# Layer 2's recurrence: two pairs of heads in the same slot, three units apart, equal shapes side by side, 18 slots a period

## The chip, the cores and the metric

One core of a Trainium2 chip runs the whole kernel. The metric is the device time of one execution in microseconds (us). Lower is better.

## The reference

A four-layer recurrent decoder makes one inference step: 272 prompt rows (16 of them learned meta rows) and 8 sample sequences of 8 rows each, 336 rows of 1024 features. Layer 2, the one that is changed, is an RWKV-7 time mixer with 32 heads of 64 features. Cut to what matters:

```python
def rwkv_chunk(p, carry, xn, pos0):
    ...
    def step(s, inp):
        r_t, w_t, k_t, v_t, a_t, b_t = inp
        sa = jnp.einsum('bhvk,bhk->bhv', s, a_t)
        s = s * w_t[:, :, None, :] + sa[..., None] * b_t[:, :, None, :] + v_t[..., None] * k_t[:, :, None, :]
        return s, jnp.einsum('bhvk,bhk->bhv', s, r_t)

    s_new, y = lax.scan(step, s0.astype(F32), (tm(r), tm(decay), tm(k), tm(v), tm(-kk), tm(kk * a)))
    ...
    out = (yn + bonus).reshape(b, l, D_INNER).astype(xn.dtype) * g
    return (xn[:, -1].astype(x_prev.dtype), s_new.astype(s0.dtype)), out @ p['w_o']
```

All of it is float32. The state s of one head is 64 by 64.

## The kernel before

The 32 heads are 16 pairs; the two heads of a pair lie in the two halves of the 128 partitions. The 336 columns of a pair are cut into six units of 64 (the last one padded): unit 0 holds the 64 sample columns, units 1 to 5 the prompt. Inside a unit the time steps are solved in closed form by small matrix products that were made earlier; from unit to unit the state is carried on. This is `recur(p)`. For each unit u of a pair it does, in this order:

- pX: a matmul for each head (from the packed state and values `sv` and the stored products `G`) into one corner of the bank `pch`; ScalarE copies it out as `xs`. Units 2 to 5 contract over 128 partitions (the trace writes 128*64), units 0 and 1 over 64 (64*64). Unit 0 adds two more matmuls.
- pyR (units 2 to 5): a 64*64 matmul for each head, the state's part of the output, into `pY`; and `sd`, two activations of ScalarE that scale the old state.
- pA: a 64*64 matmul for each head from `xs` and `Z` into `pch`; ScalarE copies the two halves over the state in `sv`.
- pS (units 1 to 5): a 128*64 matmul for each head from the new `sv` into `pch`; VectorE adds `sd` with a decay and writes the state of the next unit (two operations). py: a 128*64 matmul for each head into `pY`. Unit 0 also has pyI, 64*64, the sample states' part of the output.

In the trace pX and pS both stand as `pch<-SV,Gr`, pA as `pch<-xs,Zr`, pyR as `pY<-Pr,SV`, py as `pY<-Gr,SV`. Every matmul of float32 has two passes, so two heads make four records ("x4"). Three groups of work go in between:

- `before(p)`, two pairs ahead: the projection `pvv` (24 matmuls of 128 by 128 weights on 336 columns, eight steps of three), two sets of twelve 32*32 matmuls (`pAZ`), the sample products pX0 in two halves of four 128*64 matmuls, ScalarE's copy of `pvv` to `s.v` (in the trace `VF<-pvv`), three transposes `pvt` of `s.v`, and copies.
- `sample(p)`: two products by GpSimd, two 128*64 matmuls `pD` on 512 columns, the sample states.
- `after(p)`: normalization and gate of the pair before: `pb`, `pm`, `pq` (128*128) and work on the other engines. `weights` splits the next projection's weight in two parts (`whi`, `wlo`), and in the first seven periods `lanes` runs an inversion on VectorE (`tmpi`, `LT`).

The order is written out by hand: `InOrder` keeps each engine's instructions in the order in which the program makes them. Time is cut into slots; `PLAN` says in which slot of a period each step of a helper is made. The recurrence of a pair runs over two periods. In each slot first the recurrence makes its step or steps, then the helpers make theirs:

```python
        for q in (p, p + 1):
            if 0 <= q < KE and t % 2 == q % 2:
                next(us[q])
        later(t)
```

So before, pair p (units 3 to 5) and pair p + 1 (units 0 to 2) take turns, the one in the even slots and the other in the odd ones, three steps a unit, 20 slots a period. There are 17 periods, numbered p = -1 to 15 here; p = -1 has one pair only, and in periods 14 and 15 the projection of layer 2's output stands where `before` stood.

Of the kernel before, what the change touches and what calls it, by code (L numbers as in the profile page):

```python
# [10 lines left out]
F32 = mybir.dt.float32  # L11
# [6 lines left out]
P = 128  # L18
# [3 lines left out]
KE = E // P  # L22
# [5 lines left out]
N = NSAM + NP  # L28
# [20 lines left out]
CH = 64  # L49
NU = 6  # L50
NB = 384
# [187 lines left out]
class K:  # L239
# [12 lines left out]
    "products": (9, 10, 11, 12, 13, 14, 15),  # L252
    "chain": (7, 8, 9, 11, 12, 13, 13, 17, 17, 18, 19, 21, 22, 23, 24),
    "mix": (9, 10, 11, 12, 12, 14, 16, 16),
    "slots": 20,
    "before": (0, 0, 0, 2, 3, 5, 6, 7, 8, 11, 11, 13, 14, 16, 18, 19),
    "weights": (6, 7, 8, 14),
    "after": (0, 3, 6, 9, 11, 16, 17, 19, 19, 21, 25),
    "lanes": (3, 5, 14, 16, 19),
    "pz": (0, 1, 2, 6, 8, 12, 12, 13),  # L260
    "begun": (14, 14, 15, 15, 16, 17, 18, 19),
    "last": (4, 5, 6, 7, 8, 9, 10, 11, 14, 15, 16, 17),
    "wlo": (0, 1, 0, 1, 0, 1, 0, 1, 0, 1),
    "fill": (2, 2, 2, 3, 2, 3, 3, 3, 3, 3, 3),
    "tail": (0, 0, 0, 1, 0, 1, 1, 1, 1, 1, 1),
    "sample": (6, 10, 18, 19, 19, 19),
}


# [159 lines left out]
def blocks(t):  # L429
    return [t[:, j] for j in range(t.shape[1])]  # L430
# [866 lines left out]
def layer2(k, O):  # L1297
    nc, tc, A = k.nc, k.tc, k.A
# [20 lines left out]
    ss = [slice(0, HD), slice(HD, P)]  # L1319
    vs = ss[::-1]  # L1320
# [274 lines left out]
    def plan(g, start, slots):  # L1595
        for t in slots:
            todo.setdefault(start + t, []).append(g)

    def later(t):
        for g in todo.pop(t, ()):  # L1600
            next(g, None)
# [4 lines left out]
    for n in range(2 * KE + 2):  # L1606
        p, t0 = n // 2, 8 * n
# [5 lines left out]
        if p == KE:  # L1613
            x = gh, gl
            pgs.append(out)
        else:
            x = xr if n % 2 else xk
# [44 lines left out]
    lanes = [invert(n) for n in range(1, 4 * KE * NU // P)]  # L1662
# [50 lines left out]
    def before(p, x=None):  # L1713

        s = st[p]
        if p:
            pvv = k.ps.tile([P, 512], F32, tag="mm", name="pvv")[:, :N]
            x = dense_steps(k, pvv, W[p], blocks(vh), blocks(vl))
        else:
            x = iter(())  # L1720
        ab = Ab[p % 2]
        for hp in range(2):
            nc.gpsimd.tensor_copy(ab[ss[hp], :, hp], s.A0[ss[hp]].rearrange("p w (b t) -> p b w t", t=TS))
        for _ in range(3):
            next(x, None)
            yield

        pAZ = k.ps.tile([P, 512], F32, tag="az", name="pAZ")
        n = NU * HB
        A_ = tw.tile([P, NU, HB], F32, tag="A_", name="A_", bufs=1)  # L1730
        for u in range(NU):
            for hp in range(2):
                nc.tensor.matmul(pAZ[low[hp], u * HB : (u + 1) * HB], s.L[top[hp], u], s.Z[top[hp], u, HB:], start=True, stop=True)
        yield
        for hp in range(2):
            nc.vector.tensor_copy(A_[low[hp]].rearrange("p u c -> p (u c)"), pAZ[low[hp], :n])
        yield
        next(x, None)
        yield
        for u in range(NU):  # L1740
            for hp in range(2):
                nc.tensor.matmul(pAZ[top[hp], n + u * HB : n + (u + 1) * HB], A_[low[hp], u], s.Z[low[hp], u, HB:], start=True, stop=True)
        yield
        next(x, None)
        for hp in range(2):
            nc.vector.tensor_copy(s.Z[top[hp], :, HB:], pAZ[top[hp], n : 2 * n].rearrange("p (u c) -> p u c", c=HB))
        yield
        for _ in range(3):
            next(x, None)
            yield  # L1750
        pX0 = k.ps.tile([P, 512], F32, tag="az", name="pX0")[:HD, : NS * 4 * TS]
        s.x0 = tw.tile([P, 2, NS, TS], F32, tag="x0", name="x0")
        for half in range(2):
            for b in range(half * NS // 2, (half + 1) * NS // 2):
                nc.tensor.matmul(pX0[:, b * 4 * TS : (b + 1) * 4 * TS], s.S0[:, b], ab[:, b].rearrange("p g w t -> p (g w t)"), start=True, stop=True)
            if half == 0:
                if p:
                    nc.scalar.copy(s.v[:, :N], pvv)
            yield
        pvt = k.ps.tile([P, 512], F32, tag="mm", name="pvt")[:, :NB]  # L1760
        for j in range(3):
            nc.tensor.transpose(pvt[:, j * P : (j + 1) * P], s.v[:, j * P : (j + 1) * P], k.ident)
        for hp in range(2):
            nc.scalar.copy(s.x0[vs[hp]].rearrange("p w b t -> p b w t"), pX0.rearrange("p (b g w t) -> p b g w t", g=2, w=2, t=TS)[:, :, hp])
        yield
        for j in range(2):
            for hp in range(2):
                nc.vector.tensor_copy(s.sv[vs[hp], j::2, hp], pvt[ss[j]].rearrange("p (u g c) -> p u g c", g=2, c=HD)[:, :, hp])
            yield

    NT = PLAN["slots"]

    def recur(p):

        s = st[p]
        sv, G = s.sv, s.G
        s.c = k.ps.tile([P, 512], F32, tag=f"c{p % 2}", name="pch")
        pX, pA, pS = (s.c[:, j * HD : (j + 1) * HD] for j in (0, 0, 1))
        for u in range(NU):
# [4 lines left out]
                    nc.tensor.matmul(pX[ss[hp]], s.x0[vs[hp], 1].rearrange("p b t -> p (b t)"), k.ident[vs[hp], vs[hp]], start=False, stop=True)  # L1784
            xs = tw.tile([P, HD], F32, tag="xs", name="xs", bufs=2)
            nc.scalar.copy(xs, pX)
            if u > 1:
                py = [s.Y[h, u * CH : (u + 1) * CH] for h in ss]
                sd = tw.tile([P, HD], F32, tag="sd", name="sd", bufs=2)
                for hp, h in enumerate(ss):  # L1790
                    nc.tensor.matmul(py[hp], sv[h, u, hp], s.R[h, u], start=True, stop=False)
                    nc.scalar.activation(sd[h], sv[h, u, hp], AF.Copy, scale=WC[h, p, NS + u - 1 : NS + u])
            yield
            for hp in range(2):
                nc.tensor.matmul(pA[ss[hp]], s.Z[ss[hp], u], xs[ss[hp]], start=True, stop=True)
            for hp, h in enumerate(ss):
                nc.scalar.copy(sv[h, u, hp], pA[h])
            yield
            if u > 0:
# [7 lines left out]
                for h, q in zip(ss, o):  # L1807
# [2 lines left out]
                        nc.vector.tensor_scalar(q, pS[h], d, None, op0=MUL)  # L1810
                    else:
                        nc.vector.scalar_tensor_tensor(q, pS[h], d, sd[h], op0=MUL, op1=ADD)
            if u == 0:
                s.Y = k.ps.tile([P, 512], F32, tag="Y", name="pY")[:, :NB]
            py = [s.Y[h, u * CH : (u + 1) * CH] for h in ss]
            if u == 0:
                for hp in range(2):
                    nc.tensor.matmul(py[hp], k.ident[vs[hp], vs[hp]], s.x0[vs[hp], 0].rearrange("p b t -> p (b t)"), start=True, stop=False)
            for hp in range(2):
                nc.tensor.matmul(py[hp], sv[:, u, hp], G[:, 1, hp, u], start=u == 1, stop=True)  # L1820
            if u == NU - 1:
                nc.sync.dma_start(O["wkv_p"][:, p], wo)
            yield
        for _ in range(NT - 3 * NU):
            yield

    def sample(p):
# [135 lines left out]
    todo, pz = {}, []  # L1963
# [9 lines left out]
    us, n_begun = {}, 0  # L1973
    for t in range((KE + 1) * NT):
        i, p = t % NT, t // NT - 1
        if i == 0:
# [20 lines left out]
                plan(sample(p + 1), t, PLAN["sample"])  # L1997
            if p < 6:
                plan(lanes[1], t, PLAN["lanes"])
        for q in (p, p + 1):  # L2000
            if 0 <= q < KE and t % 2 == q % 2:
                next(us[q])
        later(t)
        if p + 1 == KE:
            if i == PLAN["begun"][0]:
                begun = [dense_steps(k, pz[m], W[KE + j], yh, yl, k0) for j, m, k0 in ((3, 2, 0), (2, 0, 8))]
# [10 lines left out]
    lanes = [weights(KE + 6), weights(KE + 7)]  # L2017
# [319 lines left out]
```

## Time and profile before

| | |
|---|---|
| time, median of 3 runs | 1894.67 us (1892.24 to 1909.81) |
| the profiled execution: its own time, its span | 1909.75 us, 1908.0 us |
| mean granted TensorE clock, share of 2.4 GHz | 0.952 |
| busy share of the span: TensorE matmul, VectorE, ScalarE, GpSimd | 93%, 62%, 41%, 34% |
| the chain that ended last: TensorE, VectorE, ScalarE | 77%, 10%, 4% |

The engines run side by side, each through its own list. PE is TensorE's matmuls, PEld its weight loads, DVE VectorE, ACT ScalarE, POOL GpSimd. The chain that ended last is followed back from the last instruction, at each step to what released it.

### The profile page before, as it was taken

What the parts mean: (1) busy time and instruction counts of PE and PEld (TensorE: products, weight loads), DVE (VectorE), ACT (ScalarE), POOL (GpSimd) and SP (SyncE); (2) the same over time, 40 slices, a digit from 0 to 9 for tenths busy, and PEclk for the clock granted to TensorE, in tenths of its full rate; (3) what the DMA queues carried; (4) which work ended last, traced back from release to release, by engine and by line L of the source; (5) the groups of instructions that cost most, each with busy time, mean ns of one, the idle gap of its engine ahead of it and who ended that gap; (6) DMA issues with size and microseconds to landing.
All of it is one profiled execution on the core that took longest, in us unless ns stands there. A gap on an engine that the chain in (4) does not pass through costs nothing.

```text
span 1908.0 us, 31685 instructions
## 1 busy us (share of the span) xinstructions
PE 1775.5 (93%) x11822; PEld 1358.8 (71%) x11822; DVE 1191.0 (62%) x2234; ACT 780.7 (41%) x1789; POOL 647.9 (34%) x853
## 2 busy tenths in 40 slices
PE   5998897999789997999998999999998899999997
PEld 3665696766469996666666876677778667677777
DVE  8989546499945456556876847665545635355444
ACT  2553244321044343444345354576664324232332
POOL 5667335200000035343434333343446313132212
PEclk9999898999989998999997998899999899999999
DMA  5564544554554442356655855455524466566552
GB/s 191 139 176 129 126 145 151 174 173 137 147 135 159 141 147 77 112 188 196 188 184 167 243 174 160 141 171 179 160 90 150 135 205 206 190 196 223 173 177 73
DMA packets 198698, 306.63 MB, mean 161 GB/s; under 512 B 115504, under 2 KB 132656, under 8 KB 196048
## 3 DMA queue, kind: packets, MB, share of 16 engines
q1 hardware_dynamic: 177584, 265.86, 45.9%
q0 software_dynamic: 10400, 32.72, 5.3%
q10 hardware_dynamic: 10560, 6.03, 1.1%
q8 instruction: 93, 1.52, 0.3%
q14 instruction: 61, 0.50, 0.1%
HBM read 225.31 MB, written 79.24 MB: 160 GB/s over the span
## 4 chain that ended last, share of the span: by engine, by line
PE 77%; DVE 10%; ACT 4%; issue 3%; DMA 2%; POOL 2%; SPq 1%; ACTq 0%; POOLq 0%; DVEq 0%
PE pg L382 8%; PE pkr L382 8%; PE pu L382 6%; PE pz L448 4%; PE pz L449 4%; PE pz L450 4%; PE pgm L382 4%; PE pch L382 4%; PE pvv L382 4%; PE py L2234 3%; PE pz L382 2%; PE py L382 2%; PE pY L382 2%; PE pn L2246 1%; PE pg L448 1%
## 5 line engine op out<-in xcount | busy, mean ns | idle before, releaser
L411 DVE TENSOR_TENSOR wlo<-wst,whi 128x1024 fp32r<-128x1024 f32 x138 | 170.8, 1238 | 140.9 <-ACT whi L407 106.9
L407 ACT CAST whi<-wst 128x1024 fp32r<-128x1024 f32 (+1 forms) x125 | 129.3, 1035 | 104.8 <-PE pr L450 51.2
L382 PE MATMUL pg<-x_n,wst 128*128 128x336 f32 x512 | 163.5, 464 | 0.0
L382 POOL TENSOR_TENSOR wlo<-wst,whi 128x512 fp32r<-128x512 f32 (+1 forms) x57 | 76.2, 1338 | 159.3 <-ACT whi L382 156.2
L382 PEld LDWEIGHTS pg<-x_n,wst 128*128 128x128 f32 x512 | 94.5, 193 | 43.9 <-issue 2.5
L2247 DVE SCALAR_TENSOR_TENSOR s<-s,pn 128x512 f32<-128x512 f32 x64 | 44.0, 687 | 126.0 <-PE pn L2246 126.0
L382 PE MATMUL pu<-x_n,wst 128*128 128x336 f32 x352 | 115.0, 467 | 2.4 <-DVE x_n L491 1.8
L382 PE MATMUL pkr<-xr,wst 128*128 128x336 f32 x256 | 99.2, 484 | 0.0
L382 PEld LDWEIGHTS pu<-x_n,wst 128*128 128x128 f32 x352 | 67.6, 198 | 36.2 <-issue 3.2
L382 PEld LDWEIGHTS pgm<-AR,BK 64*128 64x128 f32 x384 | 59.6, 194 | 45.4 <-issue 25.3
L382 ACT CAST whi<-wst 128x256 fp32r<-128x256 f32 (+1 forms) x117 | 67.0, 586 | 51.0 <-issue 13.4
L382 DVE TENSOR_TENSOR G<-pgm,gmask 128x128 f32<-128x128 f32 x192 | 46.4, 284 | 63.2 <-PE pgm L382 63.0
L382 PE MATMUL pgm<-AR,BK 64*128 64x128 f32 x384 | 82.2, 321 | 1.3 <-ACT G L382 1.3
L569 POOL TENSOR_TENSOR sums<-sums 128x336 f32<-128x336 f32 x19 | 22.6, 1203 | 167.8 <-ACT sums L567 164.4
L382 PE MATMUL pkr<-xk,wst 128*128 128x336 f32 x256 | 75.9, 446 | 0.0
L2248 POOL DMA_DIRECT2D out_ret_s<-s x32 | 17.3, 540 | 165.2 <-DVE s L2247 157.8
L382 PEld LDWEIGHTS pch<-SV,Gr 128*64 128x64 f32 (+1 forms) x704 | 38.7, 141 | 43.3 <-DVE SV L382 13.4
L382 PE MATMUL pch<-SV,Gr 128*64 128x64 f32 (+1 forms) x704 | 63.1, 251 | 6.8 <-DVE SV L382 5.1
L450 PE MATMUL pz<-gh,whi 128*128 128x336 f32 x208 | 65.9, 317 | 0.0
L449 PE MATMUL pz<-gl,whi 128*128 128x336 f32 x208 | 65.8, 316 | 0.0
L448 PE MATMUL pz<-gh,wlo 128*128 128x336 f32 x208 | 65.8, 316 | 0.0
L382 PEld LDWEIGHTS pkr<-xk,wst 128*128 128x128 f32 x256 | 48.6, 190 | 23.7
(779 smaller groups left out, 5337.3 us busy)
## 6 DMA issues: line engine op xcount, KB each, us to landing
wst<-in_l_in SPq DMA_DIRECT2D x64, 512.0 KB, 3.9
dG<-G SPq DMA_DIRECT2D x16, 1152.0 KB, 5.2
s<-in_l_s SPq DMA_DIRECT2D x33, 512.0 KB, 3.6
wst<-in_l_out SPq DMA_DIRECT2D x32, 512.0 KB, 3.8
wst<-in_l_glu SPq DMA_DIRECT2D x32, 512.0 KB, 3.7
wst<-in_l_g SPq DMA_DIRECT2D x32, 512.0 KB, 4.3
wst<-in_l_v SPq DMA_DIRECT2D x32, 512.0 KB, 4.8
out_ret_s<-s POOLq DMA_DIRECT2D x32, 512.0 KB, 3.9
```

The lines of the kernel that those rows point to most:

```text
L382: return lambda *a, **kw: tc.keep_in_program_order(getattr(e, name)(*a, **kw))
L407: k.nc.scalar.copy(hf, st)
L411: e.tensor_tensor(lf[:, a:b], st[:, a:b], hf[:, a:b].bitcast(F32), op=ALU.subtract)
L448: k.nc.tensor.matmul(out, lo[:, j, :], xh[kk], start=first, stop=False)
L449: k.nc.tensor.matmul(out, hi[:, j, :], xl[kk], start=False, stop=False)
L450: k.nc.tensor.matmul(out, hi[:, j, :], xh[kk], start=False, stop=last)
L569: (nc.vector if m == KD - 1 and name != "xx" else nc.gpsimd).tensor_tensor(sums[name], sums[name], t, op=ADD)
L2234: nc.tensor.matmul(read.py0[32 * c : 32 * c + 32], qs[:, d, b], states[h * NS + b][:, d], start=d == 0, stop=d == 1)
L2246: nc.tensor.matmul(pn, KS[r, j, d * P : (d + 1) * P], VS[r, j], start=True, stop=True)
L2247: nc.vector.scalar_tensor_tensor(s[:, d], s[:, d], math.exp(TS * LOG_G[h]), pn, op0=MUL, op1=ADD)
L2248: nc.gpsimd.dma_start(O["ret_s"][h, b], s)
```

## The change

`recur` now has six steps a unit and not three. In each even slot both pairs make two steps in turn: p, p + 1, p, p + 1; in odd slots neither makes one. A unit still takes three even slots: first pX of both pairs, then `sd` of both; next pA of both, then pyR or pyI and the copies to `sv` of both; last pS and the state of both, then py of both. pyR stood next to pX and now stands behind pA. A period has 18 slots. `before` gets one more step: two projection steps are now made between the halves of pX0, and the copy of `pvv` to `s.v` is made behind the second half, not the first. The slots of all helpers are set anew.

```diff
--- before.py
+++ after.py
@@ -252,18 +252,18 @@
     "products": (9, 10, 11, 12, 13, 14, 15),
     "chain": (7, 8, 9, 11, 12, 13, 13, 17, 17, 18, 19, 21, 22, 23, 24),
     "mix": (9, 10, 11, 12, 12, 14, 16, 16),
-    "slots": 20,
-    "before": (0, 0, 0, 2, 3, 5, 6, 7, 8, 11, 11, 13, 14, 16, 18, 19),
-    "weights": (6, 7, 8, 14),
-    "after": (0, 3, 6, 9, 11, 16, 17, 19, 19, 21, 25),
-    "lanes": (3, 5, 14, 16, 19),
-    "pz": (0, 1, 2, 6, 8, 12, 12, 13),
-    "begun": (14, 14, 15, 15, 16, 17, 18, 19),
+    "slots": 18,
+    "before": (1, 1, 2, 3, 5, 5, 7, 8, 9, 9, 10, 11, 11, 12, 13, 14, 15),
+    "weights": (5, 7, 8, 13),
+    "after": (0, 3, 4, 9, 10, 15, 16, 17, 17, 19, 22),
+    "lanes": (3, 5, 9, 11, 17),
+    "pz": (1, 1, 5, 5, 7, 9, 11, 13),
+    "begun": (13, 13, 15, 15, 16, 16, 17, 17),
     "last": (4, 5, 6, 7, 8, 9, 10, 11, 14, 15, 16, 17),
     "wlo": (0, 1, 0, 1, 0, 1, 0, 1, 0, 1),
     "fill": (2, 2, 2, 3, 2, 3, 3, 3, 3, 3, 3),
     "tail": (0, 0, 0, 1, 0, 1, 1, 1, 1, 1, 1),
-    "sample": (6, 10, 18, 19, 19, 19),
+    "sample": (4, 7, 16, 16, 17, 17),
 }
 
 
@@ -1721,7 +1721,7 @@
         ab = Ab[p % 2]
         for hp in range(2):
             nc.gpsimd.tensor_copy(ab[ss[hp], :, hp], s.A0[ss[hp]].rearrange("p w (b t) -> p b w t", t=TS))
-        for _ in range(3):
+        for _ in range(2):
             next(x, None)
             yield
 
@@ -1735,27 +1735,29 @@
         for hp in range(2):
             nc.vector.tensor_copy(A_[low[hp]].rearrange("p u c -> p (u c)"), pAZ[low[hp], :n])
         yield
-        next(x, None)
-        yield
+        for _ in range(3):
+            next(x, None)
+            yield
         for u in range(NU):
             for hp in range(2):
                 nc.tensor.matmul(pAZ[top[hp], n + u * HB : n + (u + 1) * HB], A_[low[hp], u], s.Z[low[hp], u, HB:], start=True, stop=True)
         yield
-        next(x, None)
         for hp in range(2):
             nc.vector.tensor_copy(s.Z[top[hp], :, HB:], pAZ[top[hp], n : 2 * n].rearrange("p (u c) -> p u c", c=HB))
         yield
-        for _ in range(3):
-            next(x, None)
-            yield
+        next(x, None)
+        yield
         pX0 = k.ps.tile([P, 512], F32, tag="az", name="pX0")[:HD, : NS * 4 * TS]
         s.x0 = tw.tile([P, 2, NS, TS], F32, tag="x0", name="x0")
         for half in range(2):
             for b in range(half * NS // 2, (half + 1) * NS // 2):
                 nc.tensor.matmul(pX0[:, b * 4 * TS : (b + 1) * 4 * TS], s.S0[:, b], ab[:, b].rearrange("p g w t -> p (g w t)"), start=True, stop=True)
             if half == 0:
-                if p:
-                    nc.scalar.copy(s.v[:, :N], pvv)
+                for _ in range(2):
+                    yield
+                    next(x, None)
+            elif p:
+                nc.scalar.copy(s.v[:, :N], pvv)
             yield
         pvt = k.ps.tile([P, 512], F32, tag="mm", name="pvt")[:, :NB]
         for j in range(3):
@@ -1784,15 +1786,23 @@
                     nc.tensor.matmul(pX[ss[hp]], s.x0[vs[hp], 1].rearrange("p b t -> p (b t)"), k.ident[vs[hp], vs[hp]], start=False, stop=True)
             xs = tw.tile([P, HD], F32, tag="xs", name="xs", bufs=2)
             nc.scalar.copy(xs, pX)
+            yield
+            if u == 0:
+                s.Y = k.ps.tile([P, 512], F32, tag="Y", name="pY")[:, :NB]
+            py = [s.Y[h, u * CH : (u + 1) * CH] for h in ss]
             if u > 1:
-                py = [s.Y[h, u * CH : (u + 1) * CH] for h in ss]
                 sd = tw.tile([P, HD], F32, tag="sd", name="sd", bufs=2)
                 for hp, h in enumerate(ss):
-                    nc.tensor.matmul(py[hp], sv[h, u, hp], s.R[h, u], start=True, stop=False)
                     nc.scalar.activation(sd[h], sv[h, u, hp], AF.Copy, scale=WC[h, p, NS + u - 1 : NS + u])
             yield
             for hp in range(2):
                 nc.tensor.matmul(pA[ss[hp]], s.Z[ss[hp], u], xs[ss[hp]], start=True, stop=True)
+            yield
+            for hp, h in enumerate(ss):
+                if u > 1:
+                    nc.tensor.matmul(py[hp], sv[h, u, hp], s.R[h, u], start=True, stop=False)
+                if u == 0:
+                    nc.tensor.matmul(py[hp], k.ident[vs[hp], vs[hp]], s.x0[vs[hp], 0].rearrange("p b t -> p (b t)"), start=True, stop=False)
             for hp, h in enumerate(ss):
                 nc.scalar.copy(sv[h, u, hp], pA[h])
             yield
@@ -1810,18 +1820,11 @@
                         nc.vector.tensor_scalar(q, pS[h], d, None, op0=MUL)
                     else:
                         nc.vector.scalar_tensor_tensor(q, pS[h], d, sd[h], op0=MUL, op1=ADD)
-            if u == 0:
-                s.Y = k.ps.tile([P, 512], F32, tag="Y", name="pY")[:, :NB]
-            py = [s.Y[h, u * CH : (u + 1) * CH] for h in ss]
-            if u == 0:
-                for hp in range(2):
-                    nc.tensor.matmul(py[hp], k.ident[vs[hp], vs[hp]], s.x0[vs[hp], 0].rearrange("p b t -> p (b t)"), start=True, stop=False)
+            yield
             for hp in range(2):
                 nc.tensor.matmul(py[hp], sv[:, u, hp], G[:, 1, hp, u], start=u == 1, stop=True)
             if u == NU - 1:
                 nc.sync.dma_start(O["wkv_p"][:, p], wo)
-            yield
-        for _ in range(NT - 3 * NU):
             yield
 
     def sample(p):
@@ -1997,9 +2000,11 @@
                 plan(sample(p + 1), t, PLAN["sample"])
             if p < 6:
                 plan(lanes[1], t, PLAN["lanes"])
-        for q in (p, p + 1):
-            if 0 <= q < KE and t % 2 == q % 2:
-                next(us[q])
+
+        for _ in range(2 - 2 * (i % 2)):
+            for q in (p, p + 1):
+                if 0 <= q < KE:
+                    next(us[q])
         later(t)
         if p + 1 == KE:
             if i == PLAN["begun"][0]:
```

## Rows read from the trace of the kernel before

**Rows 1.** Busy time by engine: the recurrence, then two periods without `lanes`; PEclk, DMA share, GB/s last.
```profile
core 0: us, PE busy (x) PEld busy (x) DVE busy (x) ACT busy (x) POOL busy (x), PEclk, DMA share, GB/s
...
1118.00:1427.00 309.00, 298.64 (x3512) 218.75 (x3512) 183.17 (x458) 189.89 (x646) 120.55 (x130) 0.93 0.48 147
...
1316.55:1349.84 33.29, 33.12 (x437) 24.03 (x435) 19.44 (x51) 22.31 (x79) 14.05 (x16) 1.00 0.57 179
```

**Rows 2.** Timeline of PE in one period: start, length, instruction, count.
```profile
1309.59 0.29 PE L382 MATMUL pY<-Gr,SV 128*64 128x64 f32 x4
1309.71 0.29 PE L382 MATMUL pch<-SV,Gr 128*64 128x64 f32 x4
...
1310.19 0.42 PE L382 MATMUL pvv<-xvh,wlo 128*128 128x336 f32 x1
...
1311.31 0.34 PE L382 MATMUL pch<-SV,Gr 128*64 128x64 f32 x4
1311.57 0.33 PE L382 MATMUL pY<-Pr,SV 64*64 64x64 f32 x4
1311.73 0.28 PE L382 MATMUL pch<-xs,Zr 64*64 64x64 f32 x4
1311.95 0.65 PE L382 MATMUL pX<-Ab,S 128*64 128x32 f32 x8
1312.53 0.33 PE L382 MATMUL pch<-xs,Zr 64*64 64x64 f32 x4
...
1314.22 0.55 PE L382 MATMUL pvt<-ident,VF 128*128 128x128 f32 x3
```

**Rows 3.** Timeline of ACT in the same period.
```profile
1311.73 0.20 ACT L382 COPY xs<-pch 128x64 f32<-128x64 f32 x1
1311.83 0.71 ACT L382 ACTIVATE sd<-SV,WC 64x64 f32<-64x64 f32 x2
1312.57 0.42 ACT L382 COPY SV<-pch 64x64 f32<-64x64 f32 x2
1313.02 0.44 ACT L382 COPY VF<-pvv 128x336 f32<-128x336 f32 x1
...
1313.81 0.41 ACT L382 CAST whi<-wst 128x256 fp32r<-128x256 f32 x1
1314.24 0.53 ACT L382 COPY x<-pX 64x128 f32<-64x128 f32 x2
```

**Rows 4.** Timeline of DVE early in the recurrence.
```profile
1167.60 0.74 DVE L382 TENSOR_TENSOR tmpi<-LT 128x255 f32<-128x255 f32 x1
1168.38 1.15 DVE L382 TENSOR_TENSOR LT<-LT,tmpi 128x255 f32<-128x255 f32 x1
...
1169.87 0.57 DVE L382 SCALAR_TENSOR_TENSOR SV<-pch,WC,sd 64x64 f32<-64x64 f32 x2
```

**Rows 5.** Timeline of PEld, its longest waits in the recurrence; in brackets idle time and releaser.
```profile
1146.86 0.20 PEld L382 LDWEIGHTS pch<-SV,Gr 128*64 128x64 f32 x4 [1.61 <-DVE SV L382]
...
1170.49 0.20 PEld L382 LDWEIGHTS pch<-SV,Gr 128*64 128x64 f32 x4 [1.70 <-DVE SV L382]
...
1212.07 0.20 PEld L382 LDWEIGHTS pch<-SV,Gr 128*64 128x64 f32 x4 [1.53 <-DVE SV L382]
...
1240.67 0.19 PEld L382 LDWEIGHTS pch<-xs,Zr 64*64 64x64 f32 x4 [1.84 <-ACT xs L382]
...
1407.26 0.29 PEld L382 LDWEIGHTS pch<-SV,Gr 128*64 128x64 f32 x4 [2.15 <-DVE SV L382]
```

**Rows 6.** Busy time in stretches of one granted clock each.
```profile
1120.00:1171.60 51.60, 48.21 (x651) 34.72 (x650) 36.38 (x92) 27.89 (x103) 21.16 (x23) 1.00 0.48 142
1171.80:1188.70 16.90, 16.90 (x133) 12.32 (x132) 8.46 (x23) 7.78 (x26) 3.53 (x3) 0.50 0.30 76
...
1212.70:1229.60 16.90, 16.90 (x135) 12.99 (x136) 7.05 (x22) 8.11 (x28) 3.56 (x4) 0.50 0.37 103
1229.80:1407.10 177.30, 172.08 (x2166) 122.86 (x2164) 103.77 (x263) 120.88 (x413) 75.20 (x83) 1.00 0.50 159
1407.30:1413.90 6.60, 6.60 (x35) 5.42 (x35) 1.23 (x3) 4.17 (x13) 2.91 (x3) 0.50 0.53 165
```

## The prediction

> **What bounds the kernel now.** I read the stretch of the recurrence first, 309 us of the 1908.0 us span, for nothing else is touched. TensorE is busy in 298.64 of the 309.00 us, ScalarE in 189.89, VectorE in 183.17 [rows 1]. Two periods late in the stretch, without the inversion on VectorE, take 33.29 us, 16.64 a period, with TensorE busy in 33.12 [rows 1]: there TensorE's list sets the time and everything else hides beside it. So I read next how TensorE's list costs its time, in the order of its starts [rows 2]. What is to be seen is that the price of two small matmuls hangs on their neighbours. A group of four records between two others of another tile shape takes 0.26 us to the next start (1311.31 to 1311.57). The first of two groups of one shape takes 0.16 (1311.57 to 1311.73), the last 0.22 (1311.73 to 1311.95), one in the middle 0.12 (1309.59 to 1309.71). Two groups side by side thus take 0.38 and apart 0.52: each change of shape that goes saves 0.14 us. Last I read ScalarE's list in the same period [rows 3], because the change moves its instructions, and the longest waits of TensorE with the clock behind them [rows 5, 6].
>
> **What is removed: changes of shape.** I wrote TensorE's list of a period out from the slots, before and after, and counted the places where a matmul's tile shape differs from that of the one ahead. Before there are 32 and 30 in turn. After there are 20: pA of both pairs, pyR and pyI stand in one run, pS and py of both in another, the halves of pX0 and both pD stand beside 128*64 groups. Periods 0 to 13 lose 154 changes, the three at the ends 22, together 505 to 329. 172 of the 176 lie between small shapes; the visits to 128*128 stay eight a period. 176 x 0.14 = **24.6 us** if nothing else becomes late; in a period of the middle 11 x 0.14 = 1.54. At half clock a change costs more, so this errs low by little.
>
> **What is moved: ScalarE's order in slots 12 to 14.** Here I find the gain again as a wait. In slot 12 the recurrence makes pX of both pairs (units 5 and 2) and their two `xs`, then `sd` of both, which is four activations. Only behind them does `before` make the second half of pX0 and the copy of `pvv` to `s.v`. In slot 13 stands `pvt`, which reads `s.v`, and behind it on TensorE is everything of slots 14 to 16. Count from the start T of that pX. The first `xs` starts 0.42 later (1311.31 on TensorE to 1311.73 on ScalarE, [rows 2, 3]; ScalarE had work until then, so at most that). The second follows some 0.12 later, T + 0.54, as its group ends so much later. `sd` starts 0.10 behind an `xs` (1311.73 to 1311.83) and two take 0.72 with their gap: four are out at T + 0.64 + 1.44 = T + 2.08. The copy takes 0.44 [rows 3]: T + 2.52. A released matmul starts 0.05 later (two state updates end at 1169.87 + 0.57 = 1170.44, the matmul behind them starts at 1170.49, [rows 4, 5]): `pvt` at T + 2.57. TensorE gets there at T + 0.16 + 0.12 for the two pX and 0.58 for the half of pX0 (1311.95 to 1312.53, [rows 2]), T + 0.86. It waits **1.71 us**. Before, one pair's two `sd` stood ahead of the copy, and it ended at 1313.46, 0.76 ahead of `pvt` at 1314.22 [rows 2, 3]: a wait of that kind did not exist.
>
> Behind the wait come `pvt` (about 0.46, estimated from three matmuls and a change of shape), four 64*64 groups (0.16 + 0.12 + 0.12 + 0.22 = 0.62) and `pq` (about 0.5, from six matmuls of 336 columns in 1.12, 1310.19 to 1311.31), so pS of pair p could start at T + 4.15 and that of p + 1 0.16 later. ScalarE's `whi` (0.41) and `x` (0.53) are done by T + 3.5, but the four copies to `sv` cannot start before the third 64*64 group is done, now that pyR reads the old state just ahead of them: about T + 3.75, and two take 0.42. The second pair is released near T + 4.6, a wait of 0.3. Together **2.0 us a period**, in the 14 periods that have both pairs and a `pvt`: 28 us. Bounds: 1.2 (the two `xs` earlier, the second wait gone) to 2.2, so 17 to 31.
>
> **What is moved and hides.** In slots 0 and 6 only pair p has `sd`, and the same walk leaves pA 0.7 us to spare; VectorE's state update ends 0.5 us and more ahead of the next pX; pX behind the last pS is covered by py and both pD, about 1.5 us, to within 0.1. SyncE's loads stay at slot 0, and a period of about the same length brings none closer to its use; `wkv_p` goes out a step later, read by nobody: 0. GpSimd's list keeps its order but for `sample`, whose products are now ready well before `pD`: 0. If one of these covers failed, the price is one of 0.1 to 0.5 a period, 1 to 7 us. VectorE's inversion has its steps in other slots. One step takes up to 0.74 + 1.15 = 1.89 [rows 4] and delays a state update behind it, both before and after. I take 0, bounds -6 and +6: one such step less or more on the way in the three periods with the large ones.
>
> **The sum, and the clock.** Without the clock: -24.6 + 28 = +3.4. The profiled execution took 1909.75 us, 1908.0 of span and 1.75 around it, 15 over the median of 1894.67. Rows 6 show two stretches of the recurrence at a granted clock of 0.50 (1.2 GHz) of about 17 us each. There TensorE started 133 matmuls in 16.90 us, 7.9 per us, against 437 / 33.29 = 13.1 at 2.4 GHz [rows 1, 6]: 16.9 x (1 - 7.9 / 13.1) = 6.7 us lost in each, 13.4 in both, close to the 15. I therefore make the sum on 1909.75 - 13.4 = 1896.4, and take the median, 1894.7, as a run without them. What went ahead of them: five times in this stretch the weight load stood idle for over 1.5 us [rows 5]. Behind 1170.49, 1212.07 and 1407.26 the clock fell to 0.50 within a us or two, behind 1146.86 and 1240.67 it stayed at 1.00 [rows 5, 6]. The change puts 14 waits of that length in, one a period, with short matmuls around them, so falls are likelier than before. I take one more than in the median run: 1894.7 + 3.4 + 6.7 = 1904.8, **1905 us**.
>
> A rule of the Trainium skill speaks against the change here. The page "TensorE: Matmul & The Clock Gate", Part 3, "The mechanism", says that matmuls start and end strictly in program order, only weight loads being pulled ahead. By that rule nothing of slots 14 to 16 can fill the wait for `s.v`, which stays whole. The five waits agree: the weight load itself stood still up to 2.15 us.
>
> **The rivals.** (1) **The clock falls often, slower.** The mechanism is the wait for `s.v` once a period, and then 1.2 GHz for some 17 us, about one period. For: three of five such waits did it. Against: at half clock TensorE gets to `pvt` later and the wait shrinks, and some falls were short (6.6 us at 1407.3). Every second or third wait of the 14 makes five falls: 1894.7 + 3.4 + 5 x 6.7 = 1932. It decides from the third fall on (1918). (2) **The wait does not bind, faster.** If `s.v` is ready when TensorE comes to `pvt`, because ScalarE has run ahead or a later matmul goes first, the 24.6 stays: 1870; with 0.7 of the wait left, 1880. For: TensorE's busy share, and that ScalarE is busy only 22.31 of 33.29 us. Against: ScalarE's list is in program order [rows 3], and `xs` cannot be earlier than its pX, so there is nothing to run ahead with. (3) **The price of a change of shape is not saved**, because waits for data and the drain overlapped: then +28 without the gain, 1922, in the slower case.
>
> **How the numbers follow.** A measurement of this kernel can tell about 1% from no change, 19 us: 1876 to 1914. The main case, gain and wait about equal and at most two falls, spans 1885 to 1913 and has 0.42. The slower cases, 1914 to 1945, have 0.38; the faster, 1862 to 1876, have 0.20. Of these I leave out the ends: 1868 to 1938, which also takes in the bounds of the wait (17 to 31) and of the inversion (-6 to +6).
>
> **What would show it.** Right: TensorE's count of matmuls unchanged, groups at 0.12 in runs of four; `pvt` with an idle of 1.5 to 1.9 us ahead, released by ScalarE's `VF`; in a full-clock period 16.5 to 17.1 us. The clock's row tells the case. Wrong: `pvt` without a wait and a period near 15.1 us would mean that I put ScalarE's queue wrongly; a period over 18 us at full clock, another cover that failed, most likely VectorE's state update or the copies to `sv`.

## The result and the profile after

The changed kernel takes 1929.66 us (median of 4 runs, 1925.10 to 1931.09), the kernel before 1897.85 beside it: a ratio of 1.0128 on record, with a 95% interval of 1.0092 to 1.0164. (The eight times themselves give 1.0155 by their means and 1.0168 by their medians; the four of before are spread over 17.6 us.) Run again beside other runs of before, as `after_again` below, it stands at 1.0120 (1.0073 to 1.0167). It is slower by 1.2 to 1.7%, and inside the range that was given. The profiled execution took 1931.09 us, with a span of 1929.3 and a mean granted clock of 0.946. Its span is 21.3 us longer than that of before; from the first to the last matmul into `pch`, 22.7 us longer. So the recurrence is the place, as before. First its windows before and after, columns as in [rows 1]:

```profile
1118.50:1423.60 305.10, 294.74 (x3487) 215.03 (x3487) 181.43 (x455) 187.95 (x641) 119.52 (x129) 0.93 0.48 148
```

```profile
1115.80:1443.60 327.80, 277.50 (x3487) 206.62 (x3487) 181.04 (x455) 192.31 (x641) 120.91 (x129) 0.90 0.45 138
```

TensorE does the same 3487 matmuls in 17.2 us less busy time. But the time in which it stands idle goes from 305.10 - 294.74 = 10.4 to 50.3 us: 39.9 more. And the mean clock falls from 0.93 to 0.90. With two levels, 1.00 and 0.50, that is a share of 0.14 and then 0.20 of the stage at 1.2 GHz, 43 and 66 us. What TensorE waited for in the stage after (total in us, times, longest):

```profile
PE pvt L382 <- ACT VF L382: 25.5, 15, 2.2
PE pY L382 <- DVE cl L382: 9.2, 11, 2.3
PE pch L382 <- ACT SV L382: 9.1, 19, 1.2
PE pch L382 <- DVE SV L382: 2.8, 8, 0.6
PE pch L382 <- ACT xs L382: 1.7, 2, 1.2
```

In before the same view has 5.1 us for the state update, 1.6 for `xs`, 0.7 for the copies to `SV`, and neither of the first two rows. The first row is the predicted wait. The second was not predicted: pyI writes the bank `pY`, which is free only when VectorE's `cl` of the pair before has read it. One late period on TensorE (start, length, in brackets idle time and releaser), to be set beside [rows 2]:

```profile
1300.99 0.45 PE L382 MATMUL pch<-SV,Gr 128*64 128x64 f32 x8
1301.27 0.60 PE L382 MATMUL pX<-Ab,S 128*64 128x32 f32 x8
1303.59 0.55 PE L382 MATMUL pvt<-ident,VF 128*128 128x128 f32 x3 [1.72 <-ACT VF L382]
1304.07 0.61 PE L382 MATMUL pch<-xs,Zr 64*64 64x64 f32 x8
1304.46 0.65 PE L382 MATMUL pY<-Pr,SV 64*64 64x64 f32 x8
1305.46 0.65 PE L382 MATMUL pch<-cl,ob 128*128 128x336 f32 x1 [0.36 <-ACT SV L382]
```

and ScalarE in the same place, beside [rows 3]:

```profile
1301.37 0.35 ACT L382 COPY xs<-pch 128x64 f32<-128x64 f32 x2 [1.49 <-PE pch L382]
1301.62 1.46 ACT L382 ACTIVATE sd<-SV,WC 64x64 f32<-64x64 f32 x4
1303.10 0.44 ACT L382 COPY VF<-pvv 128x336 f32<-128x336 f32 x1
```

Both pX stand side by side now, as one group of 8 in 0.28 us (1300.99 to 1301.27), where before each of them stood alone at 0.26 or as a first at 0.16. But with T = 1300.99 the four `sd` end at T + 2.09 and the copy `VF` at T + 2.55, and `pvt` starts at T + 2.60. It could have started at T + 0.88.

The clock, in short stretches around this `pvt` and the next:

```profile
1303.80:1304.10 0.30, 0.30 (x5) 0.13 (x3) 0.00 (x0) 0.28 (x2) 0.06 (x1) 1.00 0.00 0
1304.30:1310.80 6.50, 6.14 (x53) 4.08 (x50) 4.16 (x11) 3.01 (x11) 1.89 (x3) 0.50 0.58 157
1311.20:1323.09 11.89, 10.17 (x161) 8.06 (x160) 5.14 (x14) 7.46 (x27) 4.46 (x6) 1.00 0.52 163
...
1324.80:1327.90 3.10, 3.10 (x22) 1.74 (x24) 1.47 (x5) 1.32 (x4) 0.01 (x1) 0.50 0.86 229
```

TensorE stands idle for 1.72 us, starts `pvt` at 2.4 GHz, and within 0.6 us of that start the clock is at 1.2 GHz for some 7 us. A period later the same, for some 3.4 us. In the whole stage there are 14 such falls, and 12 of them begin within 2.5 us of the start of one of the 16 `pvt`. The other two come with an idle of 2.33 us at pyI and one of 1.19 us at the last `pq`. None is as long as the stretches of 17 us of before [rows 6]. A late period takes 18.7 to 19.9 us, against 16.64 [rows 1].

### The profile page after: what moved, and what is told of

It is laid out like the page before. It is cut to its first block, busy times and chain, and to the rows that moved or that the text cites. A ratio compares the mean times of both kernels' runs of the same rounds, so it can differ in the third digit from the quotient of the medians.

```text
span 1929.3 us, 31775 instructions
## 1 busy us (share of the span) xinstructions
PE 1757.9 (91%) x11822; PEld 1350.1 (70%) x11822; DVE 1190.1 (62%) x2234; ACT 785.6 (41%) x1789; POOL 646.0 (33%) x853
## 3 DMA queue, kind: packets, MB, share of 16 engines
q8 instruction: 93, 1.52, 0.3%
## 4 chain that ended last, share of the span: by engine, by line
PE 73%; DVE 12%; ACT 6%; issue 4%; DMA 2%; POOL 2%; SPq 0%; ACTq 0%; DVEq 0%; POOLq 0%
PE pg L382 8%; PE pkr L382 8%; PE pu L382 6%; PE pz L448 4%; PE pz L449 4%; PE pz L450 4%; PE pgm L382 4%; PE pch L382 3%; PE py L2239 3%; PE pvv L382 2%; PE pz L382 2%; PE py L382 2%; PE pn L2251 1%; PE pg L448 1%; PE pv L382 1%
## 5 line engine op out<-in xcount | busy, mean ns | idle before, releaser
L382 PE MATMUL pch<-SV,Gr 128*64 128x64 f32 (+1 forms) x704 | 53.4, 260 | 4.9 <-DVE SV L382 2.8
```

Source lines behind the costliest of these rows:

```text
L382: return lambda *a, **kw: tc.keep_in_program_order(getattr(e, name)(*a, **kw))
```

## The experiments

Three questions were open. Is it the waits alone, or the falls of the clock as well, and does the one bring the other? What stands next when the wait for `s.v` is taken away? And is the gain from fewer changes of shape there at all? Each expectation says in its own words which theories it tells apart. Edits are against the changed kernel. What is called a late period here runs from one `pvt` to the next, behind the last step of `lanes`.

**after_again**: the changed kernel as it is, for the spread of its falls.

> The changed kernel as it is, on the chip of these runs, for comparison: 1.009 to 1.016 of the kernel before, a fall of the clock in nearly every period.

1928.82 us; the stage again 327.7 us, the mean clock in it again 0.90, with 12 falls. Two late periods in a row had no fall, with the same wait of 1.72 us at `pvt`:

```profile
1345.60:1363.30 17.70, 14.88 (x217) 11.17 (x218) 9.33 (x25) 11.31 (x40) 7.00 (x8) 1.00 0.61 169
1363.30:1381.00 17.70, 14.89 (x217) 11.18 (x217) 9.33 (x25) 11.29 (x40) 7.00 (x8) 1.00 0.51 164
```

This separates the terms within one execution. At 2.4 GHz TensorE is busy for 14.88 us where it was 33.12 / 2 = 16.56 [rows 1]: 1.68 us gained a period. It is idle for 2.82: 1.72 at `pvt`, 0.46 at `pq`, 0.51 at pyI by its rows, and some 0.15 at the next pX. Waits cost more than shapes give back, by 17.70 - 16.64 = 1.06 us. And a period with a fall takes 18.7 (a short one) to 19.9 (a long one), so the fall costs another 1.0 to 2.2.

**e1_fill** and **e5_fill7**: TensorE gets work to do in the wait, matmuls of the identity with itself into unused columns of `pvt`'s bank. They add work that no output needs. e1 has 15 of them, e5 has 7.

```diff
-        pvt = k.ps.tile([P, 512], F32, tag="mm", name="pvt")[:, :NB]
+        pvt = k.ps.tile([P, 512], F32, tag="mm", name="pvt")
+        for _ in range(15 if p > 1 else 0):
+            nc.tensor.matmul(pvt[:, NB:], k.ident, k.ident, start=True, stop=True)
+        pvt = pvt[:, :NB]
```

> The changed kernel with 15 matmuls added ahead of pvt in the periods with two pairs: identity by identity, 128 columns, into columns of the pvt bank that nobody reads. They are there to keep TensorE at work through the 1.75 us in which it waits for ScalarE's copy of pvv, and take about 1.5 us; all work of the changed kernel remains. Theory A (the idle wait lowers the granted clock once a period, and the half clock is most of the loss): the clock stays at 1.00 through most of the recurrence, a period falls from 19.4 to some 17.3 us, the time by about 28 us to about 1902, although work was added. Rival B (the waits themselves are the loss, the falls have other causes): falls stay once a period, the time stays at 1930 or rises by up to 5.

e1 took 1939.50 us, a ratio of 1.0182 (1.0130 to 1.0235): slower than the change itself. The fill was mis-sized. It is 30 records in 3.46 us (1323.18 to 1326.64 on TensorE's timeline), twice the wait, so it set the period itself, 19.33 us (below, a window that is a little wider than one late period):

```profile
1323.18 3.62 PE L382 MATMUL pvt<-ident 128*128 128x128 f32 x30
1326.64 0.49 PE L382 MATMUL pvt<-ident,VF 128*128 128x128 f32 x3
```

```profile
1284.50:1303.90 19.40, 18.29 (x250) 14.61 (x248) 9.34 (x25) 11.38 (x40) 7.00 (x8) 1.00 0.53 155
```

Its time says nothing on the wait. But its clock does: 1.00 through every late period. So it was done again with a fill that fits, e5.

> As e1_fill, but with 7 added matmuls, not 15: there each took 0.23 us and not 0.1, 3.46 us in all, twice the wait of 1.72, so the fill became the bound. Seven take 1.6 us and fit into the wait. The sums go by 19.33 us a period in e1_fill at a clock of 1.00. Theory A (half clock after the idle wait is the loss): the clock stays up in the late periods, which take 19.33 - 1.75 = 17.6 us or less, against 19.4 in the changed kernel, and the time falls by 20 to 28 us to 1.00 to 1.003 of the kernel before. Rival B (the waits are the loss): falls stay and the ratio stays at 1.012 to 1.016.

TensorE's timeline of e5, then the window of one late period:

```profile
1316.32 1.83 PE L382 MATMUL pvt<-ident 128*128 128x128 f32 x14
1318.11 0.55 PE L382 MATMUL pvt<-ident,VF 128*128 128x128 f32 x3
1319.73 0.42 PE L382 MATMUL pch<-cl,ob 128*128 128x336 f32 x1 [0.46 <-ACT SV L382]
...
1324.77 0.33 PE L382 MATMUL pY<-x,ident 64*64 64x64 f32 x4 [0.52 <-DVE cl L382]
```

```profile
1298.60:1316.30 17.70, 16.59 (x233) 12.82 (x231) 9.34 (x25) 11.29 (x40) 7.00 (x8) 1.00 0.59 168
```

`pvt` stands as late as before and everything behind it too: a period of 17.70 us, that of the changed kernel without a fall, to the hundredth. The falls are gone from all late periods, with only the idle time taken away. So it is shown that the idle ahead of `pvt` brings them, though not every time, as the two periods of `after_again` show. Five falls are left in the stage, four of them with waits of 1.97 to 2.36 us at pyI in the early periods. The stage takes 316.9 us against 327.8, and the whole 1924.36 us, 1.0091 (1.0059 to 1.0123): neither theory A's 1.00 to 1.003 nor rival B's 1.012 and more. That is less than the stage gained: in this profile the part behind the stage took 490.7 us (1923.1 - 1432.4) against 485.7 in that of the changed kernel, with nothing edited there. Whether it was so in the other runs is not seen.

**e2_copy_early**: the copy of `pvv` is made at the end of slot 11, ahead of `xs` and `sd` and not behind them.

```diff
             if half == 0:
                 for _ in range(2):
                     yield
                     next(x, None)
-            elif p:
-                nc.scalar.copy(s.v[:, :N], pvv)
+                if p:
+                    nc.scalar.copy(s.v[:, :N], pvv)
```

> The changed kernel with ScalarE's copy of pvv made at the end of slot 11, ahead of slot 12's xs and sd, not behind them; nothing else. Theory A (what is too long is ScalarE's whole list between pX of slot 12 and the copies to sv of slot 14, 3.8 us for a stretch in which TensorE has 2.6): pvt no longer waits, but the wait comes back at pq or pS, some 1.2 to 2 us; the time stays within 10 us of 1930. Rival B (only the place of the copy was wrong): the wait is gone, the clock stays up, a period takes 15.5 to 16.5 us and the time falls by 40 us or more, to 1880 to 1890.

1910.40 us, 1.0012 (0.9978 to 1.0046). `pvt` starts without a wait, and the wait comes back three groups later, at `pq`, which writes the bank that ScalarE's four copies still read (TensorE's timeline, then the window of two late periods):

```profile
1278.14 0.55 PE L382 MATMUL pvt<-ident,VF 128*128 128x128 f32 x3
...
1280.81 0.42 PE L382 MATMUL pch<-cl,ob 128*128 128x336 f32 x1 [1.51 <-ACT SV L382]
```

```profile
1278.10:1312.10 34.00, 29.68 (x437) 22.35 (x435) 18.68 (x50) 22.16 (x79) 14.01 (x16) 1.00 0.60 177
```

So ScalarE's list from `xs` to the last copy is the limit, not the copy of `pvv` alone. Only 0.66 us of idle a period is won (idle (34.00 - 29.68) / 2 = 2.16, against 2.82). But 1.51 us of idle at this place brought one fall in the late periods, where 1.72 at `pvt` brought one nearly each time. That the place comes back was expected for the case that ScalarE sets the time; that the time would then stay was wrong, for the clock stayed up.

**e6_pvt14**: the last three steps of `before` one slot later, so that pA and pyR of both pairs stand ahead of `pvt` on TensorE.

```diff
-    "before": (1, 1, 2, 3, 5, 5, 7, 8, 9, 9, 10, 11, 11, 12, 13, 14, 15),
+    "before": (1, 1, 2, 3, 5, 5, 7, 8, 9, 9, 10, 11, 11, 12, 14, 15, 16),
```

> The changed kernel with pvt and what hangs on it one slot later (slots 14, 15, 16 for 13, 14, 15): pvt then stands behind pA and pyR of both pairs, which need only xs. One wait of 1.72 us becomes two of about 1 us, ahead of pvt and ahead of pq, with 1 us of matmuls between. Theory A: the sum of waits falls by 0.3 to 0.5 us a period, but above all no single wait is long, so most falls go: a late period takes 16.6 to 17.2 us, the ratio is 0.995 to 1.005. Rival B (the length of the single wait is not what counts, only their sum): the falls stay in most periods, the ratio stays above 1.01.

1909.03 us, 1.0011 (0.9979 to 1.0043). The wait is split in two, 1.33 us together, and the late periods come down to 17.0 us with one fall of the clock among them (TensorE's timeline):

```profile
1274.21 0.55 PE L382 MATMUL pvt<-ident,VF 128*128 128x128 f32 x3 [1.11 <-ACT VF L382]
1274.98 0.42 PE L382 MATMUL pch<-cl,ob 128*128 128x336 f32 x1 [0.22 <-ACT SV L382]
```

The sum of the idle time fell too, from 2.82 to 2.0 us a period, so the late periods alone do not tell the length of a wait from the sum of the waits. The early periods help: each of the four waits of 2.08 to 2.46 us at pyI has a fall in it or within 2 us behind it, and of the 14 waits of 1.08 to 1.11 us at `pvt` only two.

**e3_sd_pool**: `sd` of units 2 and 5, the four activations of slot 12, on GpSimd.

```diff
-                    nc.scalar.activation(sd[h], sv[h, u, hp], AF.Copy, scale=WC[h, p, NS + u - 1 : NS + u])
+                    if u in (2, 5):
+                        nc.gpsimd.tensor_scalar(sd[h], sv[h, u, hp], WC[h, p, NS + u - 1 : NS + u], None, op0=MUL)
+                    else:
+                        nc.scalar.activation(sd[h], sv[h, u, hp], AF.Copy, scale=WC[h, p, NS + u - 1 : NS + u])
```

> The changed kernel with the sd of units 2 and 5, the four that stand in slot 12, made by GpSimd (a multiplication by the same scalar) and not by ScalarE. Theory A: the copy of pvv ends 1.4 us earlier, pvt waits 0.3 us or less, pq waits up to 1 us; most falls of the clock go; a period takes 16 to 17 us and the time falls by 30 to 45 us, to 1885 to 1900. Rival B (GpSimd is slower at it, or stands behind its own list): the copies to sv wait for it, the wait moves to pq and pS, the time stays at 1920 to 1935.

1904.92 us, 0.9980 (0.9944 to 1.0016), level with before and 5 us above theory A's range. GpSimd takes 2.04 us for the four where ScalarE took 1.46, but nobody waits for them (TensorE's timeline, then the window of that late period):

```profile
1280.42 0.55 PE L382 MATMUL pvt<-ident,VF 128*128 128x128 f32 x3 [0.25 <-ACT VF L382]
1282.04 0.42 PE L382 MATMUL pch<-cl,ob 128*128 128x336 f32 x1 [0.46 <-ACT SV L382]
...
1287.09 0.33 PE L382 MATMUL pY<-x,ident 64*64 64x64 f32 x4 [0.50 <-DVE cl L382]
```

```profile
1280.40:1296.70 16.30, 14.90 (x218) 11.19 (x218) 9.41 (x25) 9.87 (x36) 8.75 (x12) 1.00 0.64 184
```

A late period is below that of before for the first time. What remains of the loss is early, in the periods with `lanes`: 44 us at half clock there, in four falls, each at a wait of 1.95 to 2.32 us at pyI.

**e4_pyi_late**: pyI goes back to where it stood before the change, just ahead of py of unit 0.

```diff
-                if u == 0:
-                    nc.tensor.matmul(py[hp], k.ident[vs[hp], vs[hp]], s.x0[vs[hp], 0].rearrange("p b t -> p (b t)"), start=True, stop=False)
...
+            if u == 0:
+                for hp in range(2):
+                    nc.tensor.matmul(py[hp], k.ident[vs[hp], vs[hp]], s.x0[vs[hp], 0].rearrange("p b t -> p (b t)"), start=True, stop=False)
```

> The changed kernel with pyI, the 64*64 matmuls that open unit 0's output bank, moved from behind pA in slot 2 to just ahead of py in slot 4: the bank is free only when VectorE's cl has read it, and pyI was seen to wait 0.5 us for that late and up to 2.4 us in the periods with the inversion. It adds two changes of shape a period, 4 us in all. Theory A (that wait is a cover that failed, beside the one at pvt): the wait goes, the time falls by 5 to 15 us, to 1915 to 1925. Rival B (VectorE's list is late anyway, and what comes next waits as long): the time stays within 4 us of 1930.

1929.33 us, 1.0120 (1.0066 to 1.0174): nothing won. The wait for `cl` is gone, and idle time falls by 9.5 us (327.30 - 286.51 = 40.8, against 50.3). But TensorE is busy for 9.0 us more (the window of the stage):

```profile
1116.60:1443.90 327.30, 286.51 (x3487) 213.50 (x3487) 183.22 (x455) 192.68 (x641) 120.92 (x129) 0.87 0.47 139
```

Some 2 to 4 of it are two more changes of shape a period (14 x 0.14, by the busy times of e9 and e10 below, to 14 x 0.28, by the prediction's price); the rest fits the mean clock of 0.87, a share of 0.26 at half clock, 85 us. There are 15 falls, ten of them of some 7 us, where the changed kernel had 14 and five. Why more of them were long was not settled.

**e7_pvt14_sd**: e6 and e3 together.

> e6_pvt14 and e3_sd_pool together: GpSimd makes the four sd of slot 12, and pvt stands behind pA and pyR. In e3_sd_pool a late period took 16.25 us with waits of 0.33 (pvt), 0.53 (pq), 0.49 (pyI). Theory A: the first two go, a late period takes 15.4 to 15.8 us, the ratio is 0.985 to 0.995, below both kernels. Rival B (the waits come back at the copies to sv or at pX of the next period, because ScalarE and VectorE are the bound there): 16.1 us or more and 0.995 to 1.000.

1892.37 us, **0.9930** (0.9903 to 0.9956), faster than both kernels. `pvt` and `pq` wait no more, and the late periods take 15.60 us (the window of one):

```profile
1251.40:1267.00 15.60, 14.89 (x220) 11.27 (x218) 9.32 (x25) 9.83 (x35) 8.77 (x12) 1.00 0.71 209
```

The busy time is that of the changed kernel at full clock; the gain of fewer changes of shape was there all along. What is left is in the early periods. There TensorE waits once a period like this, and the four falls of this stage are all in that part (the timelines of TensorE, then of VectorE, then of GpSimd beside it):

```profile
1200.29 0.48 PE L382 MATMUL pY<-x,ident 64*64 64x64 f32 x4 [2.29 <-DVE cl L382]
```

```profile
1197.97 0.66 DVE L382 TENSOR_TENSOR tmpi<-LT 128x175 f32<-128x175 f32 x1
1198.66 1.06 DVE L382 TENSOR_TENSOR LT<-LT,tmpi 128x175 f32<-128x175 f32 x1
1199.65 0.49 DVE L382 TENSOR_TENSOR cl<-pY,ch 128x336 fp32r<-128x336 f32 x1
```

```profile
1198.39 1.14 POOL L382 TENSOR_TENSOR S<-S,WC 128x512 f32<-128x512 f32 x1
```

pyI waits for `cl`, and `cl` stands behind the step of `lanes` in slot 17. Three kernels follow from e7. **e8_pyi** has pyI late, as in e4. **e9_lanes** moves the steps of `lanes`:

```diff
-    "lanes": (3, 5, 9, 11, 17),
+    "lanes": (0, 5, 7, 11, 13),
```

**e10_both** has both.

> e7_pvt14_sd (0.993 of before, late periods of 15.6 us) with pyI moved behind the state update of unit 0, just ahead of py0. Theory A: at full clock the wait of pyI for VectorE's cl (0.6 us in late periods, up to 2.7 in periods with the inversion) is on the path, and now goes; two more changes of shape cost 0.28 a period: late periods near 15.3, early ones 1 to 2 us shorter than in e7, ratio 0.983 to 0.991. Rival: the wait only moves to pY's next reader, as without the other two edits, and the changes of shape are paid: 0.993 to 0.998.

> e7_pvt14_sd with the inversion's steps in slots 0, 5, 7, 11, 13 in place of 3, 5, 9, 11, 17. Theory A: in the periods that have it, pyI and the next pX are late because the step of slot 17 stands ahead of cl on VectorE; without it they wait for under 1 us, an early period comes down from about 20 us to about 17.5, with fewer falls of the clock there: ratio 0.980 to 0.988; late periods unchanged at 15.6. Rival: VectorE beside GpSimd is itself the bound in those periods, the wait moves to the state update of the slot where the step now stands: 0.990 to 0.996.

> e8_pyi and e9_lanes together. If both waits are separate, the lowest of the three, 0.976 to 0.986. If the lane step was the cause of the long pyI wait, the same as e9 within 0.3% (pyI's remaining 0.6 us less two changes of shape is worth about 0.3 us in 14 periods).

| kernel | time, us | ratio (95%) | stage, us | mean clock in it | late period, us |
|---|---|---|---|---|---|
| e8_pyi | 1876.47 | 0.9835 (0.9784 to 0.9885) | 277.5 | 0.98 | 15.2 to 15.3 |
| e9_lanes | 1873.05 | 0.9816 (0.9768 to 0.9865) | 269.2 | 1.00 | 15.6 |
| e10_both | 1869.11 | 0.9800 (0.9755 to 0.9845) | 266.3 | 1.00 | 15.2 to 15.3 |

Both first theories held. In e9 the step of `lanes` on the same 175 columns takes less than half, and pyI waits for 0.6 us in the early periods as in the late ones (the timelines of VectorE and of TensorE):

```profile
1186.33 0.40 DVE L382 TENSOR_TENSOR tmpi<-LT 128x175 f32<-128x175 f32 x1
1186.75 0.36 DVE L382 TENSOR_TENSOR LT<-LT,tmpi 128x175 f32<-128x175 f32 x1
```

```profile
1192.71 0.33 PE L382 MATMUL pY<-x,ident 64*64 64x64 f32 x4 [0.62 <-DVE cl L382]
```

But VectorE is not relieved by this. The longer time now falls on another step, that of slot 0, beside the same product of GpSimd (the timelines of VectorE and of GpSimd). This step stands behind `cl`, which started at 1192.07, so pyI does not wait for it:

```profile
1192.83 1.04 DVE L382 TENSOR_TENSOR LT<-LT,tmpi 128x156 f32<-128x156 f32 x1
```

```profile
1192.48 1.21 POOL L382 TENSOR_TENSOR S<-S,WC 128x512 f32<-128x512 f32 x1
```

e10 is within 0.2% of e9: the place of the `lanes` step ahead of `cl` was the cause of the long waits, and pyI's place is worth 0.3 to 0.4 us in a late period, that is 0.6 of wait less 0.28 of two changes of shape (between e9 and e10, 0.51 less idle and 0.14 more busy time). That moving pyI paid in e8 and not in e4 goes with the clock, 0.98 and 0.87; that this is the whole reason is not shown. e10's stage:

```profile
1117.10:1383.40 266.30, 254.46 (x3486) 192.38 (x3486) 178.47 (x454) 166.77 (x577) 151.19 (x193) 1.00 0.56 171
```

Idle time is 11.8 us, close to the 10.4 of before, and the clock does not fall once.

## Why the prediction was right and where it was wrong

The range held the time, but the main case, gain and wait about equal, did not come. What came is rival (1), falls of the clock behind the new wait, at almost its time (1932) and not by its numbers. The sum was made for a run without the two long falls, 1896.4 us by the profiled execution and 1894.7 by the median; on the first base the profiled execution after, 1931.09, is 34.7 more. Both are low for a run of before: the later ones have medians of 1901.03 to 1905.27. Against those of its own comparison `after_again` is 24.0 slower (1928.82 - 1904.8), where the forecast had 10 and rival (1) had 37. So the nearness of 1932 is in part luck. The terms of the sum:

| term, us in the stage | predicted | measured |
|---|---|---|
| TensorE's busy time at 2.4 GHz (changes of shape) | -24.6 | -23.5 (estimate, 14 x 1.68) |
| waits | +28 | +39.9 |
| half clock, against a run without the long falls | +6.7 | about +20 |
| sum | +10.1 | about +36 |

The +20 is worked out: 17.2 us of busy time were saved and not 23.5, so 6.3 went to the longer time at half clock, and the base had 13.4 taken off.

**(a) Changes of shape, 0.14 us each: right.** 1.54 us were forecast for a period and 1.68 measured, in a period of the same count of matmuls at full clock. Rival (3), the price is not saved, is out, and e7 to e10 show what it is worth when nothing waits.

**(b) The wait for `s.v`: right in place, cause and size.** 1.71 us were walked out of ScalarE's list, 1.72 measured, released by `VF`; 25.5 us in 15 waits against 24 in 14. Rival (2), that it does not bind, is out. The Trainium skill, "TensorE: Matmul & The Clock Gate", Part 3, "The mechanism", has matmuls strictly in program order; the trace agrees, for nothing of the following slots started in the 1.72 us of any period. The second wait, behind it, was put at pS with 0.3; it is at `pq`, 0.46 at full clock, since `pq` needs the bank that the copies to `SV` read. That is 9.1 us of waits for `SV`, not 4.2 and the 0.7 of before.

**(c) "What is moved and hides": wrong, this is the first step that failed.** I assumed 0 for the other covers and did not walk pyI at all. Moved ahead of the state update, it needs `pY` a few groups earlier, while VectorE's `cl` still reads it: 9.2 us. It is also where the steps of `lanes` hurt, which I took as 0 with bounds of 6 either way: in slot 17 one stands ahead of `cl`. So a full-clock period takes 17.70 and not 16.5 to 17.1.

**(d) "I take one more [fall] than in the median run": wrong, the second step that failed, in count and in length.** The text itself put 14 waits of that length into the kernel and had three falls behind five such waits in before; one fall was not what these rows said. Nor were the five of that length: they were read from the weight loads, and TensorE's matmuls stood still there for 0.73 us (no fall), 1.16 and 0.99 (falls), 1.56 (no fall) and 1.87 (a fall). Two of the five, on TensorE's timeline of before:

```profile
1146.86 0.34 PE L382 MATMUL pch<-SV,Gr 128*64 128x64 f32 x4 [0.73 <-DVE SV L382]
...
1407.26 0.48 PE L382 MATMUL pch<-SV,Gr 128*64 128x64 f32 x4 [1.87 <-DVE SV L382]
```

And my price was wrong the other way: 17 us at half clock and 6.7 lost each, five of them in rival (1). In truth falls come at 12 of 16 `pvt`, last some 3.4 or 7 us, and cost 1.0 to 2.2 us. Count and length erred against each other, which is the other part of the luck in 1932. That the wait shrinks at half clock was a reason against, and it fell: the fall ends before the next `pvt`, so each wait begins at 2.4 GHz and is 1.72 again.

What stays open: why 1.51 us of idle at `pq` let the clock stand in most periods, and 1.72 at `pvt` did not. The two differ in length and in the work around them, and no run changes one alone. A count over the 13 profiles speaks for the length. Take every stretch in this stage in which TensorE's matmuls stood idle, and which began at 2.4 GHz. Of 55 stretches of 1.0 to 1.52 us, ten had a fall in them or within 2.5 us behind; of 68 of 1.69 us and more, 61 had one (a fall between two stretches counts for the longer). The kernels differ in more than these lengths, so this is not a proof. Nor was it settled why e4 has more half clock than the changed kernel.

## What to carry to other kernels

When like steps are put side by side on the busiest engine, the steps that serve them are put side by side on the others too: walk every buffer that a moved instruction writes, and every list that it now stands in, not only the one that looks tight. A wait of 1.7 us that comes back every period costs more than its length, through the clock; split it, or put it where other matmuls stand ahead (e6), before giving up the edit. A gain that seems lost can be told from one that was never there by the busy time of the same instructions in a stretch of full clock.

## What was not expected of the hardware

- One idle stretch of 1.72 us, in a period where TensorE is otherwise busy for 14.88 of 17.70 us, was followed by 1.2 GHz for 3.1 to 6.5 us or a little more in nearly every period; with 14 matmul records in the same gap the clock was 1.00 throughout. Yet the kernel before ran 177 us at 1.00 with a wait of the weight load of 1.84 us early in it [rows 5, 6], of which the matmuls stood still for 1.56.
- The same two operations of VectorE on 175 columns took 0.66 and 1.06 us in e7, where GpSimd's products `y<-y,sg` (1197.54 to 1198.44) and `S<-S,WC` (1198.39 to 1199.53) ran beside them, and 0.40 and 0.36 us in e9, where GpSimd was in its four `sd` (1184.63 to 1187.34). The Trainium skill, "SBUF — State Buffer", "SBUF: two separate sides", says that the two engines share a pair of ports, which one of them holds for a whole instruction when VectorE reads two inputs from SBUF. The first pair of rows agrees: each of the two ends 0.19 us after the one product beside it that had started first. The second does not show such a block. In the 13 profiles it is so throughout: in this stage all 123 `LT<-LT,tmpi` that started while GpSimd was in an operation on two tensors took 0.72 to 1.09 us longer than the quickest of the same size. The 35 that started while it was in a `sd` or an `Ab`, which read one tensor, and the 245 that started while it was in none took at most 0.03 longer. The two kinds of GpSimd operation differ in more than the number of tensors, so which difference counts is not shown.
